# Seven block products in place of eight for the projection of v, z, q and k in a two-layer trunk

## The chip, the cores and the metric

One Trainium2 chip, one core of it, one launch. The metric is the device time of one execution in microseconds (us); the median of several runs is given, and one further execution was recorded by the hardware profiler.

## What is computed

Two layers, 512 tokens, width 1024. Per layer (cut from the reference):

```python
h = rms_norm(x, pre_norm[layer])
proj = h @ w_in[layer]                      # 1024 -> 8192 columns
c_b, c_c, c_x, c_z, r_q, r_k, r_v, r_z = split(proj)          # 1024 columns each
y_conv = c_b * causal_depthwise_conv(c_c * c_x, conv_w[layer]) * silu(c_z)
q, k = apply_rotary(r_q), apply_rotary(r_k)                   # 8 heads of 128
ret = retention_chunkwise(q, k, r_v, log_gamma)               # chunks of 128 tokens
ret = ret * rsqrt(mean(ret * ret) + eps)                      # per head
mix = concat(y_conv, ret * silu(r_z))                         # 2048
x = x + rms_norm(mix @ w_out[layer], post_norm[layer])
```

## The kernel before

Every operand of a product with a weight is split exactly into a high and a low part (`split`, L97: ScalarE writes the high part, VectorE subtracts it and writes the low part), and every product runs as three passes, high x high, high x low and low x high (`mm3`, L251 to L254). A weight unit is 256 rows by 512 columns (512 KB); one DMA brings it (`raw`), the split makes `wh` and `wl`, in three rotating buffers each. `prepare` (L129) splits units two ahead of the one that TensorE is at, and `fetch` (L116) asks for the load three ahead.

A layer goes through four pairs of heads, then the output projection. A pair has four runs of 96 matmuls, each of 128 x 128 by 512 columns:

- [v z], with the tokens as the stationary operand (4 token tiles, 8 slices of 128 rows, 3 passes). `take_vz` (L295) scales v on VectorE and takes SiLU of z on ScalarE.
- [q k], with the weight as the stationary operand, so that q and k come out with the head dimension on partitions. `rope` (L312) turns them by the rotary tables on VectorE.
- Two runs for two tiles of 128 channels of the convolution (`conv`, L421). Beside them TensorE does the retention's small products: `scores` (L334), `state` (L358), `attend` (L371). `state` wants k with tokens on partitions; `k_natural` (L348) makes that by 32 x 32 transposes on VectorE.

`finish` (L408) transposes the pair's result y in 16 pieces on VectorE and splits it into `mTh`, `mTl`; it is traced in the hooks of the next pair's [v z] run. The output projection (L551 on) takes `mTh`, `mTl` as the stationary operand. Between the layers, `transposed` (L476) turns the new x by TensorE and splits it.

Engines work in order, each on its own queue. The program is traced in the order of the text; the framework then places each engine's instructions in a queue, by the order of tracing among those that its plan finds ready. A hook is work traced behind a step of a run.

## Time and profile before

| | us |
|---|---|
| median of 3 runs | 943.01 (942.83 to 943.49) |
| span of the profiled execution | 941.0 |
| TensorE, VectorE, ScalarE, GpSimd busy | 933.1, 596.7, 278.4, 24.6 |
| one pair (from the first `pss` of pair 0 to that of pair 1, 62.54 to 156.04) | 93.5 |

Engines are named PE (TensorE matmul), PEld (its weight load), DVE (VectorE), ACT (ScalarE), POOL (GpSimd) and SP (the queue that issues most loads). A row of a group gives line, engine, operation, output and inputs, shapes and count, then busy time, the mean in ns of one, and the idle time ahead of it with what ended it. A row of a timeline gives start, duration, engine and line. Matmuls overlap in the records (one is about 390 ns long and a new one starts every 0.23 us), so the pace of TensorE is read from starts, not from durations. Times within a run are from the start of the span.

### The profile page before, as it was taken

Reading aid. Unit: us, or ns where it says so; the run is one execution under the profiler, and the core shown is the slowest. Engines: PE = TensorE matmul, PEld = TensorE weight load, DVE = VectorE, ACT = ScalarE, POOL = GpSimd, SP = SyncE. Lnnn points to the kernel's source line nnn. Section 1 sums busy time; section 2 is a strip of 40 time slices with the busy share of each in tenths; the row PEclk is TensorE's granted clock in tenths of the full one; section 3 lists DMA queues with packets and bytes.
Section 4 is the critical chain, followed back from the end, with each engine's and each line's share of the span. In section 5 each row is a group of like instructions: output and inputs, shape, how many; then the busy total and the mean of one; then the engine's idle time right before and its main releaser. Section 6 shows DMA issues by size and latency. Waiting matters only on the chain.

```text
span 941.0 us, 10986 instructions
## 1 busy us (share of the span) xinstructions
PE 933.1 (99%) x4338; PEld 776.0 (82%) x4338; DVE 596.7 (63%) x960; ACT 278.4 (30%) x450; POOL 24.6 (3%) x46
## 2 busy tenths in 40 slices
PE   9999999999999999999999999999999999999997
PEld 6788888888888888888888888888888888888886
DVE  5595839583958395825764948394849484947324
ACT  5522331222133213324542133213321332222311
POOL 0000000000000000000000000000000000000000
PEclk9999999999999999999999999999999999999999
DMA  8522132213222322235532222322222222222222
GB/s 309 178 92 90 53 127 90 90 63 116 90 90 68 112 90 90 71 108 179 178 122 103 91 90 79 100 90 90 88 92 90 90 90 90 90 91 90 89 68 90
DMA packets 27700, 96.60 MB, mean 103 GB/s; under 512 B 3328, under 2 KB 3456, under 8 KB 27648
## 3 DMA queue, kind: packets, MB, share of 16 engines
q1 hardware_dynamic: 27504, 95.88, 30.7%
q8 instruction: 34, 0.56, 0.2%
q14 instruction: 18, 0.15, 0.1%
q10 hardware_dynamic: 144, 0.01, 0.0%
HBM read 93.78 MB, written 2.10 MB: 102 GB/s over the span
## 4 chain that ended last, share of the span: by engine, by line
PE 94%; DMA 2%; DVE 1%; ACT 1%; issue 1%; POOL 0%; SPq 0%; DVEq 0%; POOLq 0%; ACTq 0%
PE mm L252 30%; PE mm L254 29%; PE mm L253 29%; PE pa L378 2%; PE pss L339 2%; PE pa L382 1%; PE pk L361 1%; DMA xT<-in_x_t 1%; DMA x<-in_x 1%; DVE wl L100 1%; DMA pre_c<-in_pre_norm 0%; DVE x L470 0%; PE psx L481 0%; ACT wh L99 0%; ACT jx L219 0%
## 5 line engine op out<-in xcount | busy, mean ns | idle before, releaser
L100 DVE TENSOR_TENSOR wl<-raw,wh 128x1024 fp32r<-128x1024 f32 (+1 forms) x169 | 205.4, 1217 | 226.5 <-ACT wh L99 222.8
L99 ACT ACTIVATE wh<-raw 128x1024 fp32r<-128x1024 f32 (+1 forms) x169 | 178.1, 1054 | 470.6 <-PE mm L253 303.1
L252 PE MATMUL mm<-hTh,wh 128*128 128x512 f32 x768 | 302.5, 394 | 0.1
L254 PE MATMUL mm<-hTh,wl 128*128 128x512 f32 x768 | 299.8, 390 | 0.3 <-DVE wl L100 0.3
L253 PE MATMUL mm<-hTl,wh 128*128 128x512 f32 x768 | 298.7, 389 | 0.0
L254 PEld LDWEIGHTS mm<-hTh,wl 128*128 128x128 f32 x768 | 144.1, 188 | 31.4 <-DVE wl L100 0.7
L252 PEld LDWEIGHTS mm<-hTh,wh 128*128 128x128 f32 x768 | 144.3, 188 | 29.3 <-ACT z L304 0.6
L253 PEld LDWEIGHTS mm<-hTl,wh 128*128 128x128 f32 x768 | 144.3, 188 | 29.1
L252 PE MATMUL mm<-wh,hTh 128*128 128x512 f32 x256 | 99.6, 392 | 0.3 <-ACT hTh L99 0.3
L253 PE MATMUL mm<-wl,hTh 128*128 128x512 f32 x256 | 99.8, 390 | 0.0
L254 PE MATMUL mm<-wh,hTl 128*128 128x512 f32 x256 | 99.8, 390 | 0.0
L252 PE MATMUL mm<-wh,mTh 128*128 128x512 f32 x256 | 99.8, 390 | 0.0
L254 PE MATMUL mm<-wh,mTl 128*128 128x512 f32 x256 | 99.6, 389 | 0.0
L253 PE MATMUL mm<-wl,mTh 128*128 128x512 f32 x256 | 99.6, 389 | 0.0
L252 PEld LDWEIGHTS mm<-wh,hTh 128*128 128x128 f32 x256 | 48.1, 189 | 11.5 <-ACT wh L99 1.2
L415 DVE STREAM_TRANSPOSE yT<-y 32x256 f32<-32x256 f32 x128 | 55.8, 436 | 2.1
L253 PEld LDWEIGHTS mm<-wl,hTh 128*128 128x128 f32 x256 | 48.1, 188 | 10.5 <-DVE wl L100 0.6
L254 PEld LDWEIGHTS mm<-wh,mTl 128*128 128x128 f32 x256 | 48.0, 188 | 10.1
L254 PEld LDWEIGHTS mm<-wh,hTl 128*128 128x128 f32 x256 | 48.1, 188 | 9.9
L252 PEld LDWEIGHTS mm<-wh,mTh 128*128 128x128 f32 x256 | 48.1, 188 | 9.9
L253 PEld LDWEIGHTS mm<-wl,mTh 128*128 128x128 f32 x256 | 48.1, 188 | 9.9
L356 DVE STREAM_TRANSPOSE kn<-qk 32x192 f32<-32x192 f32 x128 | 47.3, 370 | 2.0
(85 smaller groups left out, 596.3 us busy)
## 6 DMA issues: line engine op xcount, KB each, us to landing
raw<-in_w_in SPq DMA_DIRECT2D x127, 512.0 KB, 3.3
raw<-in_w_out SPq DMA_DIRECT2D x40, 512.0 KB, 3.3
x<-in_x SPq DMA_DIRECT2D x4, 512.0 KB, 7.2
out<-x SPq DMA_DIRECT2D x8, 256.0 KB, 2.1
xT<-in_x_t SPq DMA_DIRECT2D x3, 512.0 KB, 7.7
post<-in_post_norm SPq DMA_DIRECT2D x2, 512.0 KB, 5.5
xT<-in_x_t SPq DMA_DIRECT2D x2, 256.0 KB, 3.9
raw<-in_w_in SPq DMA_DIRECT2D x2, 256.0 KB, 4.2
```

The lines of the kernel that those rows point to most:

```text
L99: nc.scalar.activation(out=dst_h, in_=src, func=AF.Copy)
L100: nc.vector.tensor_tensor(out=dst_l, in0=src, in1=dst_h.bitcast(F32), op=ALU.subtract)
L252: nc.tensor.matmul(out=ps, lhsT=ah, rhs=bh, start=first, stop=False)
L253: nc.tensor.matmul(out=ps, lhsT=ah, rhs=bl, start=False, stop=False)
L254: nc.tensor.matmul(out=ps, lhsT=al, rhs=bh, start=False, stop=last)
L339: nc.tensor.matmul(out=pss[:, j, :], lhsT=self.kT[:, h, s], rhs=self.qT[:, h, s], start=True, stop=True)
L356: nc.vector.transpose(out=self.kn[cols, :, :, rows], in_=src[rows, :, : NT - 1, cols])
L361: nc.tensor.matmul(out=pk[:, h, :], lhsT=self.kn[:, h, t, :], rhs=self.vs[t][:, h, :], start=True, stop=True)
L378: nc.tensor.matmul(out=pa[:, j, :], lhsT=self.sT[b][:, j, :], rhs=self.vs[t][:, h, :], start=True, stop=(t == 0))
L382: nc.tensor.matmul(out=pa[:, j, :], lhsT=self.qT[:, h, t * P : (t + 1) * P], rhs=self.S[t][:, h, :], start=False, stop=True,)
L415: nc.vector.transpose(out=self.yT[rows, :, :, cols], in_=self.y[cols, :, :, rows])
```

## The change

[v z] and [q k] of a pair become one product of a 2 x 2 block matrix (tokens in halves of 256, input rows in halves of 512) by another (input rows in halves, [v z] and [q k] as column halves), done by seven block products (Strassen's scheme) instead of eight. A block product is 24 matmuls (2 token tiles, 4 slices, 3 passes) and takes two weight entries of 12 matmuls each; a pair has 14 such entries in place of 8 of 24.

- Four of the seven take a sum of weight blocks; VectorE builds it in place in the loaded buffer (`sums` in `prepare`), ahead of the split. Fourteen entries per pair are split instead of eight. There are ten loads instead of eight, in nine rotating load buffers.
- Four take a sum of blocks of the normalised tokens; `block_sums` builds and splits these once per layer.
- Results are combined out of PSUM: three copies by ScalarE (`R[1]`, `R[7]`, `R[2]`), three additions by VectorE.
- q and k now come out with tokens on partitions. `rope` works per token tile on strided views, `k_natural` goes, and `turn` makes the transposed q and k: per token tile four transposes on TensorE into a bank of PSUM and one copy by ScalarE.
- `take_vz` is on ScalarE alone. The splits of the mixer's result move from `finish` and `conv` into `parts`, between the units of the output projection.
- In the first pair of layer 0 the first two block products need half of the tokens; `second_tokens` scales and splits the rest behind them.
- The residual x leaves its buffers: it is written out (`keep_x`) in layer 1's first pair and read again (`load_x`) ahead of the output projection; `post` is loaded there too.
- PSUM: three double banks for products and two single ones for the rest, in place of five and three.

The diff, cut:

```diff
+    mm = ctx.enter_context(tc.tile_pool(name="mm", bufs=1, space=PSUM))
+    aux = ctx.enter_context(tc.tile_pool(name="aux", bufs=2, space=PSUM))
...
+    FIRST = ("p2", "p1", "p7", "p6", "p5", "p4", "p3")
+    OTHER = ("p1", "p7", "p6", "p2", "p5", "p4", "p3")
...
+                    if prod == "p1":
+                        blk[11, u] = load(w_in[l, g, u])
+                        entry(prod, [blk[11, u]], [], blk[11, u])
+                    elif prod == "p2":
+                        blk[21, u] = load(w_in[l, g, 2 + u])
+                        entry(prod, [blk[21, u]], [], blk[21, u])
+                    elif prod == "p7":
+                        blk[12, u], blk[22, u] = load(w_in[l, g + 1, u]), load(w_in[l, g + 1, 2 + u])
+                        entry(prod, [blk[12, u], blk[22, u]], [(blk[22, u], blk[12, u], "add", blk[22, u])], blk[22, u])
+                    elif prod == "p6":
+                        entry(prod, [], [(blk[22, u], blk[11, u], "subtract", blk[22, u])], blk[22, u])
+                    elif prod == "p5":
+                        entry(prod, [], [(blk[11, u], blk[11, u], "subtract", blk[12, u])], blk[11, u])
+                    elif prod == "p4":
+                        entry(prod, [], [(blk[22, u], blk[22, u], "add", blk[21, u])], blk[22, u])
+                    else:
+                        j = load(w_in[l, g + 1, 2 + u])
+                        entry(prod, [j], [], j)
...
+            ls, sums, src = entries[i]
+            for dst, a, op, b in sums:
+                nc.vector.tensor_tensor(out=raws[dst], in0=raws[a], in1=raws[b], op=getattr(ALU, op))
             wh = wpool.tile([P, 2, 512], F32R, name=f"wh{i}", tag="wh")
             wl = wpool.tile([P, 2, 512], F32R, name=f"wl{i}", tag="wl")
...
+                split(wh, wl, raws[src])
             ws[i] = (wh, wl)
...
+    def block_sums(l, raw, Sh, Sl):
+        def blk(i, j):
+            return raw[:, 4 * (j - 1) : 4 * j, 256 * (i - 1) : 256 * i]
+        def parts(f, src):
+            split(Sh[:, f], Sl[:, f], src)
+        nc.vector.tensor_tensor(out=blk(2, 2), in0=blk(2, 2), in1=blk(2, 1), op=ALU.subtract)
+        nc.vector.tensor_tensor(out=blk(2, 1), in0=blk(2, 1), in1=blk(1, 1), op=ALU.subtract)
+        parts(1, blk(2, 1))
+        nc.vector.scalar_tensor_tensor(
+            out=blk(1, 1), in0=blk(2, 2), scalar=-1.0, in1=blk(1, 1), op0=ALU.mult, op1=ALU.subtract
+        )
+        parts(2, blk(1, 1))
+        parts(0, blk(2, 2))
+        nc.vector.tensor_tensor(out=blk(1, 2), in0=blk(1, 1), in1=blk(1, 2), op=ALU.add)
+        parts(3, blk(1, 2))
...
+        where = dict(p1=W, p6=W, p5=W, p3=W, p2=X, p7=Y, p4=Y)
...
+        def behind(prod):
+            if prod == "p1":
+                R[1] = copy("r1", W, "qk", padded_shape=[P, 4, 512])
+            elif prod == "p7":
+                R[7] = copy("r7", Y, "R", bufs=2)
+            elif prod == "p6":
+                R[2] = copy("r2", W, "R", bufs=2)
+            if prod in ("p1", "p2") and prod != order[0]:
+                nc.vector.tensor_tensor(out=R[1], in0=X, in1=R[1], op=ALU.add)
+            if prod == ("p2" if order[0] == "p1" else "p7"):
+                first_vz()
+            if prod == "p5":
+                nc.vector.tensor_tensor(out=R[7], in0=W, in1=R[7], op=ALU.add)
+                O[1] = rope(l, p, 1, R[7])
+            elif prod == "p4":
+                nc.vector.tensor_tensor(out=R[2], in0=Y, in1=R[2], op=ALU.add)
+                take_vz(l, p, 1, R[2], *VZ, *factors())
+            elif prod == "p3":
+                O[0] = rope(l, p, 0, W)
...
+        for prod in order:
+            base = at[l, p, prod]
+            for u in range(2):
+                wh, wl = ws[base + u]
+                for t in range(2):
+                    for kk in range(2):
+                        k = 2 * u + kk
+                        ah, al = operand(prod, k, t)
+                        first = prod in ("p1", "p2", "p7") and k == 0
+                        mm3(where[prod][:, t, :], ah, al, wh[:, kk, :], wl[:, kk, :], first, k == 3,
+                            prod in ("p6", "p5", "p3", "p4"))
+                step_done(base + u + 1)
+                for fn in hooks.get((prod, u), ()):
+                    fn()
+            behind(prod)
+        banks.extend((tags[1], tags[2], tags[0]))
+        return *VZ, O
...
+        def turn(self, t):
+            ps = aux.tile([P, 4, P], F32, name=f"pt_{self.tag}_{t}", tag="aux")
+            for j in range(4):
+                nc.tensor.transpose(
+                    out=ps[:, j, :], in_=self.O[t // 2][:, t % 2, j * P : (j + 1) * P], identity=ident
+                )
+            nc.scalar.activation(out=self.qkT[:, :, t * P : (t + 1) * P], in_=ps, func=AF.Copy)
...
+    def second_tokens():
+        for k in range(NK):
+            for half in (1, 0):
+                s = slice(256 * half, 256 * half + 256)
+                nc.scalar.activation(
+                    out=xT[:, k, s], in_=xT[:, k, s], func=AF.Copy, scale=pre_c[:, 0, k : k + 1]
+                )
+        for half in range(2):
+            ks = slice(4 * half, 4 * half + 4)
+            split(hTh0[:, ks, 256:], hTl0[:, ks, 256:], xT[:, ks, 256:])
...
+                    hooks["p2", 0] = [load_rest]
+                    hooks["p2", 1] = [second_tokens]
+                    hooks["p1", 0] = [lambda: block_sums(0, raw, Sh, Sl)]
+                    hooks["p7", 0] = [lambda t=t: square_sum(0, t) for t in range(NT)] + [lambda: set_factors(0)]
+                    hooks["p6", 0] = [rotary_tables]
+                else:
+                    hooks["p2", 0] = [lambda: emit(2, 0), lambda: emit(3, 0)]
+                    hooks["p2", 1] = [lambda: emit(2, 1), lambda: emit(3, 1), lambda: block_sums(1, raw, Sh, Sl)]
+                    hooks["p7", 0] = [lambda t=t: square_sum(1, t) for t in (2, 3)] + [lambda: set_factors(1)]
+                    hooks["p7", 1] = [lambda t=t: keep_x(t) for t in range(NT)]
+                hooks["p5", 0] = [lambda l=l: set_rows(l)]
+            else:
+                prods = order_of(l, p)
+                for i in range(4):
+                    hooks[prods[i // 2], i % 2] = [lambda r=done, a=i: r.finish(a)]
+            V, Z, O = seven(l, p, hTh, hTl, Sh, Sl, hooks, lambda: (fac["rx"], fac["vt"]))
+            if m is None:
+                m = [area(t, f"m{l}_{t}", [P, 8, SEQ], F32) for t in tags["m"]]
+            ret = Retention(l, p, V, Z, O, fac["et"], m)
...
+                0: [lambda t=t: ret.turn(t) for t in (2, 3, 0, 1)],
+                1: [lambda: ret.scores(0)],
+                2: [lambda: ret.scores(1)],
```

## Rows read from the trace of the kernel before

**Rows 1.** The page: busy time per engine, and the chain that ended last by engine.
```profile
PE 933.1 (99%) x4338; PEld 776.0 (82%) x4338; DVE 596.7 (63%) x960; ACT 278.4 (30%) x450; POOL 24.6 (3%) x46
...
PE 94%; DMA 2%; DVE 1%; ACT 1%; issue 1%; POOL 0%; SPq 0%; DVEq 0%; POOLq 0%; ACTq 0%
```

**Rows 2.** Waits: who waited for whom, us in total, times, longest.
```profile
PE mm L254 <- DVE wl L100: 0.3, 1, 0.3
```

**Rows 3.** Timeline of PE, 159.7 to 163.6: start, us, engine, line, operation.
```profile
159.77 0.39 PE L253 MATMUL mm<-hTl,wh 128*128 128x512 f32 x1
...
162.03 0.40 PE L254 MATMUL mm<-hTh,wl 128*128 128x512 f32 x1
...
163.08 0.48 PE L252 MATMUL mm<-hTh,wh 128*128 128x512 f32 x1
163.39 0.39 PE L253 MATMUL mm<-hTl,wh 128*128 128x512 f32 x1
```

**Rows 4.** The chain of waits, whole run: start, us, what.
```profile
62.54 0.89 PE pss L339 x8
...
156.04 0.89 PE pss L339 x8
...
455.60 0.88 PE psx L481 x8
```

**Rows 5.** Groups of instructions by shape: count, busy us, mean ns, idle before.
```profile
L100 DVE TENSOR_TENSOR wl<-raw,wh 128x1024 fp32r<-128x1024 f32 x167 | 204.1, 1223 | 226.5 <-ACT wh L99 222.8
L99 ACT ACTIVATE wh<-raw 128x1024 fp32r<-128x1024 f32 x167 | 176.8, 1059 | 470.6 <-PE mm L253 303.1 <-PE mm L254 99.4 <-issue 66.0
L323 DVE TENSOR_TENSOR qk<-t,t 128x512 f32<-128x512 f32 x32 | 22.1, 692 | 0.8
L304 ACT ACTIVATE z<-mm,rx 128x256 f32<-128x256 f32 x32 | 14.4, 472 | 20.8 <-DVE v L299 20.8
L299 DVE TENSOR_TENSOR v<-mm,vt 128x256 f32<-128x256 f32 x32 | 13.0, 421 | 11.4 <-PE mm L254 11.2
```

**Rows 6.** Stretches: busy (count) per engine, granted clock, DMA share, GB/s.
```profile
5.50:51.60 46.10, 45.62 (x198) 36.46 (x198) 27.89 (x44) 23.90 (x35) 1.29 (x2) 1.00 0.66 239
16.00:30.00 14.00, 14.00 (x63) 11.61 (x62) 4.90 (x7) 7.93 (x12) 1.16 (x1) 1.00 0.96 351
101.60:123.40 21.80, 21.80 (x98) 18.06 (x97) 18.47 (x32) 7.74 (x10) 0.10 (x1) 1.00 0.29 97
123.40:145.10 21.70, 21.70 (x97) 17.96 (x97) 8.41 (x10) 4.74 (x6) 0.00 (x0) 1.00 0.30 98
450.00:472.00 22.00, 22.00 (x107) 18.37 (x106) 17.19 (x23) 13.46 (x18) 1.10 (x2) 1.00 0.53 168
472.00:517.50 45.50, 45.22 (x209) 37.28 (x208) 24.23 (x37) 15.36 (x25) 1.67 (x3) 1.00 0.34 116
932.00:941.00 9.00, 3.03 (x14) 2.18 (x12) 5.17 (x10) 1.38 (x4) 1.09 (x2) 0.83 0.47 175
```

**Rows 7.** Timeline of DVE about the end of a pair (195.1).
```profile
141.76 0.68 DVE L320 TENSOR_TENSOR t<-mm,cos_t 128x512 f32<-128x512 f32 x1
...
192.96 1.12 DVE L403 SCALAR_TENSOR_TENSOR y<-pa,ra,z 128x128 f32<-128x128 f32 x4 [1.12 <-POOL ra L396]
...
195.60 0.42 DVE L415 STREAM_TRANSPOSE yT<-y 32x256 f32<-32x256 f32 x1
195.96 0.64 DVE L433 TENSOR_TENSOR pb<-mm,row 128x512 f32<-128x512 f32 x1
...
203.51 4.50 DVE L415 STREAM_TRANSPOSE yT<-y 32x256 f32<-32x256 f32 x10
208.04 1.23 DVE L100 TENSOR_TENSOR wl<-raw,wh 128x1024 fp32r<-128x1024 f32 x1
```

**Rows 8.** Timeline of the start: first product, last part of the transposed x.
```profile
5.50 0.98 PE L252 MATMUL mm<-wh,hTh 128*128 128x512 f32 x2
...
13.85 1.34 ACT L103 ACTIVATE hTh<-xT,pre_c 128x512 fp32r<-128x512 f32 x2 [0.21 <-DMA xT<-in_x_t]
```

More of the change, by code (lines that the diff above doesn't have):

```diff
@@ L52 @@
 C_INVF = 0
-C_MASK = C_INVF + 1
+C_MASK = C_INVF + HD // 2
 C_ID = C_MASK + P
@@ new lines, in area, with load, entry @@
+    def area(tag, name, shape, dtype):
+        return hpool.tile(shape, dtype, name=name, tag=tag)
+    loads, entries, last_use = [], [], {}
+    def load(src):
+        loads.append(src)
+        return len(loads) - 1
+    def entry(name, ls, sums, src):
+        i = len(entries)
+        entries.append((ls, sums, src))
+        for j in list(ls) + [a for t in sums for a in t if isinstance(a, int)] + [src]:
+            last_use[j] = i
+        return i
+    FIRST = ("p2", "p1", "p7", "p6", "p5", "p4", "p3")
@@ new lines, in hybrid_trunk, with fetch @@
+    NRAW = 9
+    raws, ws = {}, {}
+    with_load = {0: [(2, 0)], 1: [(3, 0)], 2: [(0, 0)], 3: [(1, 0)], 4: [(0, 1), (1, 1), (2, 1), (3, 1)]}
+    def fetch(limit):
+        done = len(ws) - 1
+        while len(raws) < len(loads):
+            j = len(raws)
+            if first_use[j] > limit or (j >= NRAW and last_use[j - NRAW] > done):
+                return
+            raws[j] = wpool.tile([P, 2, 512], F32, name=f"raw{j}", tag="raw", bufs=NRAW)
+            parts = range(2) if j == 0 else (slice(0, 2),)
+            for kk in parts:
+                for kp, half in with_load.get(j, ()):
+                    if j == 0:
+                        nc.sync.dma_start(out=xT[:, 2 * kp + kk, :256], in_=x_t[kp, half, :, kk, :])
+                    else:
+                        nc.sync.dma_start(
+                            out=xT[:, 2 * kp : 2 * kp + 2, 256 * half : 256 * half + 256], in_=x_t[kp, half]
+                        )
+                nc.sync.dma_start(out=raws[j][:, kk, :], in_=loads[j][:, kk, :])
@@ L248, in factor_rows, with mm3, bank, step_done @@
         return row, row2
-    def mm3(ps, ah, al, bh, bl, first, last):
-        nc.tensor.matmul(out=ps, lhsT=ah, rhs=bh, start=first, stop=False)
-        nc.tensor.matmul(out=ps, lhsT=ah, rhs=bl, start=False, stop=False)
-        nc.tensor.matmul(out=ps, lhsT=al, rhs=bh, start=False, stop=last)
+    def mm3(ps, ah, al, bh, bl, first, last, more=False):
+        nc.tensor.matmul(out=ps, lhsT=ah, rhs=bh, start=first, stop=False, skip_group_check=more)
+        nc.tensor.matmul(out=ps, lhsT=ah, rhs=bl, start=False, stop=False, skip_group_check=more)
+        nc.tensor.matmul(out=ps, lhsT=al, rhs=bh, start=False, stop=last, skip_group_check=more)
     cursor = [0]
+    banks = ["mm0", "mm1", "mm2"]
+    def bank(name):
+        tag = banks.pop(0)
+        return tag, mm.tile([P, 2, 512], F32, name=name, tag=tag)
+    def step_done(i):
+        cursor[0] = i
+        prepare(i + 2)
     def run_units(steps, targets, operands, hooks=None):
@@ L270, in run_units @@
                             u == 0 and kk == 0, u == n - 1 and kk == 1)
-            cursor[0] = base + min([u for later, _ in steps[i + 1 :] for u in later], default=n)
-            prepare(cursor[0] + 2)
+            step_done(base + min([u for later, _ in steps[i + 1 :] for u in later], default=n))
             for fn in (hooks or {}).get(i, ()):
                 fn()
+        banks.extend(tag for tag, _ in pairs)
         return [ps[t] for t in targets]
@@ new lines, in take_vz @@
+    def take_vz(l, p, half, src, V, Z, rx, vt):
+        for i in range(2):
+            t = 2 * half + i
+            for h in range(2):
+                s = slice(h * HD, (h + 1) * HD)
+                nc.scalar.activation(
+                    out=V[:, t, s], in_=src[:, i, s], func=AF.Copy, scale=vt[:, t, 2 * p + h : 2 * p + h + 1]
+                )
+            nc.scalar.activation(
+                out=Z[:, t, :], in_=src[:, i, 256:512], func=AF.Silu, scale=rx[:, t : t + 1]
+            )
@@ L299, in take_vz, with rope @@
+    def rope(l, p, half, src):
+        o = xpool.tile([P, 2, 512], F32, name=f"o_{l}_{p}_{half}", tag=f"x{2 + half}")
+        H = HD // 2
+        for i in range(2):
+            t = 2 * half + i
+            t1 = tpool.tile([P, 4, 2, H], F32, name=f"t1_{l}_{p}_{t}", tag="cc")
+            t2 = tpool.tile([P, 4, 2, H], F32, name=f"t2_{l}_{p}_{t}", tag="sz")
+            s4 = src[:, i, :].rearrange("p (g a d) -> p g a d", g=4, a=2)
             nc.vector.tensor_tensor(
-                out=v, in0=ps[t][:, 0:256].rearrange("p (h d) -> p h d", d=HD),
```

321 lines of the change are left out of this document (165 added, 156 removed).

## The prediction

> **What bounds the kernel now.** I read the page first. TensorE is busy 99% of the span and the chain is TensorE's to 94% [rows 1]; the waits hold nothing of weight on its side (0.3 us for a low part of a weight, once) [rows 2]. So the time is TensorE's queue, and its pace is read from starts: 10 matmuls from 159.77 to 162.03, 0.227 us each [rows 3]. The kernel has 3840 of them, 872 of 941 us. The span is 941.0, the median 943.0; 2.0 us lie around the span, and I add them at the end.
>
> VectorE has 597 busy us, 63% [rows 1], but in waves. Where a pair begins (101.6) it is busy 18.5 of 21.8 us, with the convolution's rest and `finish` of the pair ahead; then 8.4 of 21.7 [rows 6]. TensorE doesn't notice, since a unit is 24 matmuls, 5.4 us, and a split asks 1.22 us of VectorE. The change works in just these stretches.
>
> **TensorE's own sum.** Removed: 24 matmuls per pair, 192 in all, x 0.227 = 43.6 us. Added: 128 transposes in 32 calls of `turn`. The nearest row is the same operation between the layers: 8 of them 0.88 us, 0.11 each [rows 4], so 14.1 us; behind such a group the first matmul takes 0.31 instead of 0.227 [rows 3], up to 2.6 us more for 32 groups. I take 16 us, 2.0 a pair. ScalarE's copies of 512 columns out of two banks may hold up the third and fourth `turn`, a few tenths; the matmuls of the convolution stand behind. Net -27.6 us: a span of 913.4 if TensorE never waits.
>
> The page "TensorE: Matmul & The Clock Gate" of the Trainium skill, Part 4, gives about 275 ns for a transpose in a kernel's context. By it 128 would be 35 us as an estimate, and the total 19 us above mine; the row's 0.11 us is a pace, and I keep it.
>
> **VectorE in an ordinary pair (six of eight).** The 14 entries of the block product take TensorE 168 x 0.227 = 38.1 us. What must VectorE do until the last is split? From 101.6 to 145.1 it was busy 26.9 us [rows 6]. Away go: v's scaling, 4 x 0.42 = 1.7 [rows 5]; the splits of the mixer's result, 0.69 + 1.22 = 1.9 (they move to the output projection, below); rope's start from 141.76 on, 3.2 [rows 7]. Come in:
> - six more splits, 6 x 1.22 = 7.3 [rows 5];
> - eight sums of weights. No row has this very operation; `wl` has its shape, its two inputs and its engine, 1.22 [rows 5], so 9.8;
> - two of the three additions that combine (128 x 1024), 2.4;
> - rope of tokens 256 on, which is traced ahead of the last entry's split: two tiles x (0.69 + 2 x 0.42 + 0.69) = 4.4 [rows 5].
>
> Sum 26.9 - 6.8 + 23.9 = 44.0 us against 38.1. That is 5.9 too many. The two sums of p7 depend on loads alone and may run in the stretch before, where VectorE is idle half the time: 3.5 left. Neighbours that don't depend on each other overlap by some 0.09 us, which takes 1.4 off 16 of them; waits like the 1.12 us for GpSimd [rows 7] put as much back. Can it slip? A split waits for one of three buffers, so it can't run more than two entries (5.4 us) ahead; what can be put off is `finish`, 16 x 0.45 = 7.2 [rows 7], but the rows show the queue put it early: a transpose stands ahead of the convolution's product at 195.60, and ten in a row ahead of a `wl` that was ready long since (208.04) [rows 7]. That cost nothing with 5.4 us per unit; with 2.7 per entry, of which sum and split take 2.4, it does. I take 4.2 us of waiting (bounds 0 and 8: all fits, or neither p7's sums nor the overlap help). A pair: -5.4 + 2.0 + 4.2 = +0.8; six, +4.8 (-20 to +27).
>
> ScalarE, 14 splits x 1.06, three copies and v, z, comes to some 23 of 38 us [rows 5]: no bound, but it stands between a sum and its low part.
>
> **Layer 1's first pair.** From 472.0 to 517.5 VectorE had 24.2 busy us [rows 6]. To that come 7.3 + 9.8 + 2.4 + 4.4 as above, and `block_sums`, four sums and four splits of 1024 columns, 8 x 1.22 = 9.8; away go v, 1.7, and rope's start, 3.2. 53.0 us, where TensorE has 38.1 + 1.8 for the old transposes. With 1.5 us of waits in the chain of transposes, sums and splits the stage takes 54.5 instead of 45.5: +9.0, and 2.0 for `turn`: +11 (+4 to +16). `keep_x` puts four writes on SP's queue behind loads asked for four entries ahead; v of this pair waits for them on ScalarE, with splits behind it. Price 0 to 3 us, in the bounds.
>
> **Layer 0's first pair.** The first two products need tokens 0 to 255 and start as before at 5.5 [rows 8] and lose as much at the start (2.6 us: 240 matmuls, 54.4 us, lie before the first `pss` at 62.54 [rows 4]), so they end at 19. p7 needs a sum over all tokens. The last of x came at 13.9 [rows 8], with 3.5 MB asked for; in the new order some 4 MB, at about 15. Then ScalarE scales 16 pieces of 256 columns, 16 x 0.47 = 7.5 (z's row has this size and a scale by partition) [rows 5], between splits, to 22; two splits, high 1.06 and low 1.22, to 24.5; two sums to 27; the high part to 28. TensorE stands still from 19 to 28. From 27 VectorE still has 6 of the 8 block operations, six sums and eight splits (7.3 + 7.3 + 9.8), one addition, rope 4.4, and rotary tables and factors of some 5: 35 us, so the last split comes at 62 and the stage ends at 65, where [q k] ended at 51.6 (48 matmuls before that `pss`). By the same account as above: 27.9 busy [rows 6] + 33.7 - 7.7 = 54 from 5.5 with 4 to 5 idle, the same. +14, with `turn` +16 (+8 to +25).
>
> **The rest.** `parts` in the output projection: eight splits per layer where a unit of 24 matmuls leaves VectorE 4 us; nothing, with `finish` there as before. Its cover would be gone only with units of 12. Layer 1's new x is turned two steps later, four groups in 8.2 us with three splits, 5.5 + 3.7 of work: +1 (0 to 3). Loads: 16 more of 512 KB, x twice more and written once, 15 MB on 97. The start moved 351 GB/s, the pair stages under 100 [rows 6]; the densest new place is the output projection's second half with x's reload. It had 168 GB/s [rows 6]; 2.6 MB over 22 us make 290. Hidden, and `post`, now behind `finish` on SP's queue, is wanted 10 us later.
>
> **Sum.** 4.8 + 11 + 16 + 1 = +32.8 on 941.0: a span of 973.8, and 975.8 with what lies around it. 976.
>
> **Rivals.**
> 1. Hidden after all: VectorE's 44 us come down to 38, which needs 6 us per pair taken out of the stretch (finish and p7's sums done before it, rope behind the last split). For it: the stretch to 145.1 has 13 idle us in 21.7. Against it: three buffers, and a queue that puts such work first. Then only the layers' first pairs wait, about half as long: 915.4 + 1 + 5 to 15 = 921 to 931, faster. It decides where all waiting together is under 27 us; the two first pairs as I count them make 34 by themselves (14 + 5.4 and 9 + 5.4), so they would have to shrink as well.
> 2. The chain, not the work: sum (VectorE), high part (ScalarE), low part (VectorE), with VectorE idle in the 1.06 us between. Eight per pair, 8.5 us, 68 in all. For it: VectorE waited 223 us for ScalarE's half before [rows 5]; against it: when it lags, there is a next sum to fill in. Half of it gives 1010, all 1044.
> 3. In between: ordinary pairs stall 2 us, the first ones as I say less a third: 976 - 13 - 9 = 954 and down to 940.
> 4. The clock. In the last 9 us, where TensorE has work in 3.0 only, the granted clock is 0.83 [rows 6]. If it fell to the half in layer 0's standstill, each matmul behind it would cost 0.23 more: 24 of them 5.4 us, 981. It is inside the forecast's range. The same page of the Trainium skill, Part 1, has the gate throttle an idle engine; whether 9 us here do it no row shows.
>
> That the change doesn't do what it says is no case of its own: the diff fixes the count of matmuls.
>
> **Chances.** Forecast 0.65 (own range 955 to 1000; the clock lies in it), hidden 0.14, in between 0.1, the chain 0.11. The range 935 to 1008 leaves out the hidden case and, of the chain, what is above half of it. Less than 0.2% (1.9 us) the measurement can't tell from no change. Faster: 0.14 and half of the case in between, 0.19; same 0.03; slower 0.78.
>
> **What would show it.** Pair to pair (first `pss` to first `pss`) 94.3 instead of 93.5 [rows 4]; TensorE idle some 4 us in the block product of ordinary pairs, ended by `wl`, and VectorE near 9 tenths through it; TensorE idle about 9 us before p7 in layer 0. Matmul starts 0.227 apart outside the waits, 8 transposes about 0.9 us. It is wrong if the pair period is near 90 with VectorE idle there, or if VectorE waits long for ScalarE's half while TensorE waits too.

## The result and the profile after

| | before | after |
|---|---|---|
| median, us | 942.9 (942.6 to 943.5) | 988.5 (986.5 to 988.9) |
| span of the profiled execution, us | 941.0 | 986.8 |
| ordinary pair, first `pss` to first `pss`, us | 93.5 | 95.4 |

The ratio of the times is 1.048, with an interval of 1.0464 to 1.0495. The change makes the kernel 4.8% slower. 976 was forecast, in a range of 935 to 1008.

The page of the changed kernel: busy time per engine, the granted clock in 40 slices of the span, the chain that ended last.

```profile
PE 932.5 (94%) x4274; PEld 761.8 (77%) x4274; DVE 683.1 (69%) x949; ACT 398.9 (40%) x637; POOL 26.2 (3%) x46
...
PEclk9799999999999999999988999999999999999998
...
PE 75%; DVE 16%; ACT 4%; issue 3%; POOL 1%; DMA 1%; SPq 0%; DVEq 0%; POOLq 0%; ACTq 0%
```

TensorE had 94% of the chain [rows 1]; it has 75% now, and VectorE 16%. TensorE lost 192 matmuls, got 128 transposes and is as long busy as before: a busy figure doesn't tell the pace, and part of its work ran at half clock (below). To see where the 45.8 us of span lie, one looks for the same mark in both kernels. Timeline of PE, the first `pss` of pair 3 in layer 0 and of pair 0 in layer 1, before:

```profile
342.89 0.38 PE L339 MATMUL pss<-qk,qk 128*128 128x128 f32 x2
...
528.22 0.61 PE L339 MATMUL pss<-qk,qk 128*128 128x128 f32 x4
```

and after, with those of pairs 0 and 1 of layer 0 ahead of them:

```profile
83.29 0.94 PE L550 MATMUL pss<-qkT 128*128 128x128 f32 x7
178.69 0.49 PE L550 MATMUL pss<-qkT 128*128 128x128 f32 x3
...
369.69 0.49 PE L550 MATMUL pss<-qkT 128*128 128x128 f32 x3
571.42 0.49 PE L550 MATMUL pss<-qkT 128*128 128x128 f32 x3
```

| term | forecast | measured | from |
|---|---|---|---|
| layer 0's first pair | +16 | +15.3 | block product ends at 64.9 instead of 51.6 [rows 6]; `turn` 2.0 |
| six ordinary pairs | +4.8 | +11.6 | 95.4 instead of 93.5 |
| layer 1's first pair, with the new x | +12 | +16.4 | 201.7 between the marks instead of 185.3 |
| behind the last matmul | 0 | +2.2 | 8.6 us instead of 6.35 |
| sum | 32.8 | 45.5 | of 45.8 |

**An ordinary pair.** Its block product starts at 117.08 and ends at 160.28: 43.2 us, for 168 matmuls worth 38.1. Timeline of PE in it, the four waits and what follows them:

```profile
128.82 0.50 PE L346 MATMUL ps<-wl,Sh 128*128 128x512 f32 x1 [0.46 <-DVE wl L105]
...
132.12 0.51 PE L345 MATMUL ps<-wh,Sh 128*128 128x512 f32 x1 [0.47 <-ACT wh L104]
...
133.07 0.49 PE L345 MATMUL ps<-wh,hTh 128*128 128x512 f32 x1 [0.44 <-ACT wh L104]
...
134.50 0.50 PE L346 MATMUL ps<-wl,Sh 128*128 128x512 f32 x1 [0.94 <-DVE wl L105]
...
135.49 0.63 PE L346 MATMUL ps<-wl,Sh 128*128 128x512 f32 x1
135.91 0.63 PE L347 MATMUL ps<-wh,Sl 128*128 128x512 f32 x1
...
138.47 0.40 PE L347 MATMUL ps<-wh,Sl 128*128 128x512 f32 x1
138.71 0.40 PE L346 MATMUL ps<-wl,hTh 128*128 128x512 f32 x1
```

With the restarts behind them the waits make 3.6 us, all at the fifth to seventh of the fourteen entries (the 50th and the 61st to 63rd of the 168 matmuls); no wait of weight follows in the stage. Behind them eight matmuls start 0.42 us apart instead of 0.23: TensorE at the lower of its two clock levels, 1.5 us more. Timeline of VectorE ahead of the same waits:

```profile
124.79 1.22 DVE L215 TENSOR_TENSOR raw<-raw,raw 128x1024 f32<-128x1024 f32 x1
125.92 0.69 DVE L645 TENSOR_TENSOR m_E<-acc,sz 128x512 f32<-128x512 f32 x1
126.62 0.88 DVE L619 STREAM_TRANSPOSE m_E<-y 32x256 f32<-32x256 f32 x2
127.54 1.23 DVE L105 TENSOR_TENSOR wl<-raw,wh 128x1024 fp32r<-128x1024 f32 x1
128.79 0.89 DVE L619 STREAM_TRANSPOSE m_E<-y 32x256 f32<-32x256 f32 x2
129.69 1.22 DVE L215 TENSOR_TENSOR raw<-raw,raw 128x1024 f32<-128x1024 f32 x1
130.95 2.24 DVE L619 STREAM_TRANSPOSE m_E<-y 32x256 f32<-32x256 f32 x5
133.22 2.36 DVE L105 TENSOR_TENSOR wl<-raw,wh 128x1024 fp32r<-128x1024 f32 x2
```

The convolution's last step (L645), `finish` (L619), weight sums (L215) and splits (L105) stand in one queue. At 130.95 five transposes, for which nobody waits yet, stand ahead of the low parts of the sixth and seventh entry; for the first of them TensorE waits until 134.50. Twelve of the 16 transposes come in the block product before these low parts.

**The first pair of a layer.** Timeline of PE, the standstills (the first four lines are layer 0, the others layer 1):

```profile
20.66 0.39 PE L347 MATMUL ps<-wh,hTl 128*128 128x512 f32 x1
31.37 0.80 PE L345 MATMUL ps<-wh,Sh 128*128 128x512 f32 x1 [10.32 <-ACT Sh L104]
...
45.48 0.39 PE L347 MATMUL ps<-wh,Sl 128*128 128x512 f32 x1
47.95 0.50 PE L345 MATMUL ps<-wh,Sh 128*128 128x512 f32 x1 [2.07 <-ACT r L445]
...
505.34 0.40 PE L347 MATMUL ps<-wh,hTl 128*128 128x512 f32 x1
515.23 0.79 PE L345 MATMUL ps<-wh,Sh 128*128 128x512 f32 x1 [9.49 <-ACT Sh L104]
...
530.26 0.39 PE L347 MATMUL ps<-wh,Sl 128*128 128x512 f32 x1
534.07 0.52 PE L345 MATMUL ps<-wh,hTh 128*128 128x512 f32 x1 [3.43 <-ACT wh L104]
```

In both layers p7 waits for `Sh`, the high part of its own block sum, which is the second that VectorE makes. In layer 1 VectorE makes that sum at 512.87 and is busy without a pause from 502.4 until then, with the new x, its low parts, a weight sum and an addition that combines. In layer 0, p5 follows p6 on the same bank of PSUM and waits for ScalarE's copy of it (2.07). In layer 1, a weight's high part waits on ScalarE (3.43); ScalarE's timeline shows behind what:

```profile
529.46 1.05 ACT L104 ACTIVATE wh<-raw 128x1024 fp32r<-128x1024 f32 x1
532.17 0.91 ACT L500 ACTIVATE z<-r,rx 128x256 f32<-128x256 f32 x2 [1.66 <-POOL rx L323]
532.98 1.04 ACT L104 ACTIVATE wh<-raw 128x1024 fp32r<-128x1024 f32 x1
```

z stands ahead of the split and waits for `rx`, which GpSimd makes from the square sums that ScalarE itself wrote until 529.5.

### The profile page after: what moved, and what is told of

Its sections match the earlier page's. It is cut to its first block, busy times and chain, and to the rows that moved or that the text cites. A ratio compares the mean times of both kernels' runs of the same rounds, so it can differ in the third digit from the quotient of the medians.

```text
span 986.8 us, 11141 instructions
## 1 busy us (share of the span) xinstructions
PE 932.5 (94%) x4274; PEld 761.8 (77%) x4274; DVE 683.1 (69%) x949; ACT 398.9 (40%) x637; POOL 26.2 (3%) x46
## 4 chain that ended last, share of the span: by engine, by line
PE 75%; DVE 16%; ACT 4%; issue 3%; POOL 1%; DMA 1%; SPq 0%; DVEq 0%; POOLq 0%; ACTq 0%
PE mm L347 16%; PE mm L346 16%; PE mm L345 16%; PE ps L346 7%; PE ps L347 6%; PE ps L345 6%; DVE wl L105 4%; ACT wh L104 2%; PE pa L581 2%; DVE raw L215 1%; PE pss L550 1%; PE pa L586 1%; DVE m_C L619 1%; DVE m_E L619 1%; PE pk L563 1%
## 5 line engine op out<-in xcount | busy, mean ns | idle before, releaser
L105 DVE TENSOR_TENSOR wl<-raw,wh 128x1024 fp32r<-128x1024 f32 (+1 forms) x217 | 262.6, 1217 | 154.1 <-ACT wh L104 135.1
L345 PE MATMUL mm<-hTh,wh 128*128 128x512 f32 x512 | 203.8, 398 | 0.0
L347 PE MATMUL mm<-hTh,wl 128*128 128x512 f32 x512 | 201.2, 393 | 0.0
L346 PE MATMUL mm<-hTl,wh 128*128 128x512 f32 x512 | 199.5, 390 | 0.0
L345 PE MATMUL ps<-wh,Sh 128*128 128x512 f32 x256 | 107.5, 420 | 26.3 <-ACT Sh L104 20.9
L346 PE MATMUL ps<-wl,Sh 128*128 128x512 f32 x256 | 107.2, 419 | 9.5 <-DVE wl L105 9.5
L347 PE MATMUL ps<-wh,Sl 128*128 128x512 f32 x256 | 105.3, 411 | 0.2 <-DVE Sl L105 0.2
L215 DVE TENSOR_TENSOR raw<-raw,raw 128x1024 f32<-128x1024 f32 x64 | 76.9, 1221 | 33.8 <-DMA raw<-in_w_in 33.8
L345 PE MATMUL mm<-wh,mh 128*128 128x512 f32 x256 | 99.8, 390 | 0.0
L347 PE MATMUL mm<-wh,ml 128*128 128x512 f32 x256 | 99.6, 389 | 0.0
L346 PE MATMUL mm<-wl,mh 128*128 128x512 f32 x256 | 99.6, 389 | 0.0
```

The costliest lines, as they stand in the source:

```text
L105: nc.vector.tensor_tensor(out=dst_l, in0=src, in1=dst_h.bitcast(F32), op=ALU.subtract)
L215: nc.vector.tensor_tensor(out=raws[dst], in0=raws[a], in1=raws[b], op=getattr(ALU, op))
L345: nc.tensor.matmul(out=ps, lhsT=ah, rhs=bh, start=first, stop=False, skip_group_check=more)
L346: nc.tensor.matmul(out=ps, lhsT=ah, rhs=bl, start=False, stop=False, skip_group_check=more)
L347: nc.tensor.matmul(out=ps, lhsT=al, rhs=bh, start=False, stop=last, skip_group_check=more)
```

## The experiments

Two theories of the ordinary pair were on record for the first runs, "work" (VectorE has too much to do until the last split) and "chain" (sum, high part, low part, one after the other on two engines). A third, "early peak" (what VectorE has to do ahead of the first consumers sets the wait, not its total), was formed after the first four runs. The diffs are cut; their lines are those of the changed kernel. Work that is traced later is not bound to run later: the framework's plan may put it ahead of other work as soon as its operands are ready, so where an instruction stands is read from the trace of each run.

**1. `finish` traced in the convolution run.** It goes behind steps 1 and 2 of the first convolution run.

```diff
-                    hooks[prods[i // 2], i % 2] = [lambda r=done, a=i: r.finish(a)]
+            late = [lambda r=done, a=a: r.finish(a) for a in range(4)] if done else []
...
+                1: [lambda: ret.scores(0)] + late[:2],
+                2: [lambda: ret.scores(1)] + late[2:],
```

> The 16 transposes of `finish` move from the block product of the next pair into its first convolution run; nothing else changes. Theory 'work': VectorE has 44 us to do in the 38.1 us of an ordinary pair's block product, and TensorE waits for the excess. Without the 7.2 us of `finish` it has 37, so the 3.6 us of waits in an ordinary pair go, and with them the 1.5 us at half clock: pair period 90.3 to 91.5 instead of 95.4, total 958 to 965. Rival 'chain': TensorE waits for the passage sum (VectorE), high part (ScalarE), low part (VectorE), which this leaves as it is: period 94 or more, total 980 or more. The first pairs of the layers keep their time under both.

972.97 us (ratio 1.0324, 1.0294 to 1.0354), above the 958 to 965 that "work" asked for. The block product takes 39.25 us: of the 5.1 lost, 1.2 is left, and no matmul in it runs at half clock. But the rest of the pair takes 53.2 instead of 52.2, and the period is 92.4. Timeline of VectorE in the block product of this run, from 118.04 to 157.30:

```profile
131.44 2.35 DVE L105 TENSOR_TENSOR wl<-raw,wh 128x1024 fp32r<-128x1024 f32 x2
...
138.36 1.78 DVE L619 STREAM_TRANSPOSE m_E<-y 32x256 f32<-32x256 f32 x4
...
144.74 3.15 DVE L619 STREAM_TRANSPOSE m_E<-y 32x256 f32<-32x256 f32 x7
```

The transposes did not leave the block product. 15 of the 16 are in it, as in the changed kernel, but only two ahead of the low parts of the sixth and seventh entry, where the changed kernel has twelve. Of the 52 instructions that VectorE starts in the changed kernel's block product, 51 are there too (the last one of `rope` moved behind it). So the run took no work away, as its expectation took for granted; it changed the order, and the order is worth 3.9 us of the stage. That falsifies "chain", whose sums and splits are all still there, and it speaks against "work" as well. What the total does is seen behind the stage: VectorE is busy 38.8 of its 39.3 us, and 0.9 of the microsecond that the rest of the pair loses are two waits for low parts, with their restarts, where the convolution's run begins. The first pairs of the layers, expected to keep their time, are longer by 1.0 and 2.2 us.

**2. More work for VectorE.** One more addition of 128 x 512, traced ahead of each weight sum, 0.685 us by its row, 5.5 us a pair.

```diff
             for dst, a, op, b in sums:
+                scr = tpool.tile([P, 512], F32, name=f"scr{i}", tag="scr")
+                nc.vector.tensor_tensor(out=scr, in0=raws[a][:, 0, :], in1=raws[b][:, 0, :], op=getattr(ALU, op))
```

> Ahead of each of the eight sums of weights of a pair VectorE does one more addition of 128 x 512 into a scratch tile (0.60 us each where it follows an independent one), 4.8 us a pair. Theory 'work': VectorE is full in these stretches, so nearly all of it shows: period 99.5 to 100.5, total 1020 to 1030. Rival 'chain': VectorE idles while ScalarE makes the high part, and the added work fits in there at least by half: period under 98, total under 1010.

990.45 us in one run. The ordinary periods are 94.4 to 95.6 and TensorE's idle time in the stage is 3.5 to 4.4 us, so the 99.5 us that "work" forecast didn't come. But the run doesn't test what it was made for. Timeline of VectorE, an addition in an ordinary block product (217.16 to 260.35) and one in the convolution's runs behind it:

```profile
240.47 0.69 DVE L216 TENSOR_TENSOR scr<-raw,raw 128x512 f32<-128x512 f32 x1
...
278.43 0.69 DVE L216 TENSOR_TENSOR scr<-raw,raw 128x512 f32<-128x512 f32 x1 [4.90 <-DMA raw<-in_w_in]
```

Six of a pair's eight additions run in the convolution's runs, where VectorE has room, and the other two at 23 and 30 us into the block product, behind the last early wait. Not one stands ahead of the waits, and the waits are the same (0.46, 0.47, 0.45, 0.93). So the run says nothing of the total or the peak in an ordinary pair. Two things it does show. In the three ordinary pairs where the clock stayed up the block product is 42.3 to 42.5 us, where run 3 has 42.0: of the 1.4 us of the two late additions 0.3 to 0.5 show. And in layer 0's first pair all eight additions are in the block product, which takes 65.2 us, against 59.8 in the changed kernel and 60.1 to 61.0 in runs 1, 3, 5 and 11: there most of the added 5.5 us shows.

**3. Keeping TensorE busy in the standstill.** 40 matmuls of zeros ahead of p7 in each layer's first pair.

```diff
+            if p == 0 and prod == "p7":
...
+                for _ in range(40):
+                    nc.tensor.matmul(out=pz, lhsT=zz[:, :P], rhs=zz[:, :512], start=True, stop=True)
```

> In the first pair of each layer 40 products of zeros (128 x 512, 8.7 us) stand on TensorE's queue ahead of p7, where it waited 10.3 and 9.5 us. Theory: the granted clock falls to the half because TensorE stood still; with the dummies p7 starts as late as before, but at the full clock, and the 8 to 10 matmuls at 0.425 us behind each standstill take 0.227: 1.5 to 2 us less in layer 0, 1 to 2 in layer 1, total 984 to 987 by the same measure as the 988.5 of the changed kernel. Rival: what comes next is late anyway (VectorE's work sets the time), and the clock costs nothing: total within 1 us. Rival: the dummies themselves delay p7: total up by some us.

986.19 us (1.0465, 1.0415 to 1.0515), not told apart from the changed kernel. In layer 0 the matmuls are back at 0.23 us apart at 34.2 instead of 36, but the block product ends at 65.7, no earlier than 64.9: the later waits for ScalarE's copy and for weights take the gain. So the half clock behind layer 0's standstill is not on the path. The profiled span is 4.5 us shorter mostly for another reason: in three of the six ordinary pairs the half clock hardly appears, and their block product takes 42.0 instead of 43.2. In layer 1 the block product takes 58.8 instead of 60.6, but without the zeros it is anywhere from 59.1 to 62.2 in runs 1, 2, 5 and 11, so a gain there is not shown.

**4. First pairs by eight plain products.** The first pair of each layer multiplies [v z] and [q k] as before; `block_sums` moves into its [q k] run, with the second pair the first to need it. The loads of layer 0's x go back to their old order. Of the diff only the call is shown.

```diff
-            V, Z, O = seven(l, p, hTh, hTl, Sh, Sl, hooks, lambda: (fac["rx"], fac["vt"]))
+            if p == 0:
+                V, Z, O = eight(l, p, hTh, hTl, raw, Sh, Sl)
+            else:
+                V, Z, O = seven(l, p, hTh, hTl, Sh, Sl, hooks, lambda: (fac["rx"], fac["vt"]))
```

> The first pair of each layer does its eight products plainly (tokens stationary, 192 matmuls, no sums); the sums of tokens for the later pairs are made during its [q k] run. Theory: the first pairs lose 21.3 and 20.7 us to waits and half clock because the sums of tokens and weights stand between their operands and TensorE; plainly they take 43.5 us plus 2.6 at the start of layer 0 and plus 2 of transposes in layer 1, so 13 to 14 us less in layer 0 and 13 to 15 less in layer 1: total 959 to 963. Rival: the sums only move and hold up the rest of the pair: a gain under 15 us, total over 973.

962.57 us (1.0214, 1.0184 to 1.0244). The first `pss` comes at 72.3 instead of 83.3 and the distance across the layers is 187.6 instead of 201.7; the other periods are 95.2 to 95.4 as before. 25 of the 45.8 us are gone with the scheme in the two first pairs alone.

**5. The same work, later.** `finish` is issued behind p2 and p5, the fourth and fifth product; VectorE's work in the stage is the same.

```diff
-                    hooks[prods[i // 2], i % 2] = [lambda r=done, a=i: r.finish(a)]
+                    hooks[prods[3 + i // 2], i % 2] = [lambda r=done, a=i: r.finish(a)]
```

> The four finish steps of the previous pair are issued behind the steps of p2 and p5 (the fourth and fifth product) in place of those of p1 and p7 (the first two). VectorE has exactly the same work in the block product, only later. Theory 'early peak' (TensorE waits at the third to sixth entry because the conv's rest, the finish and the first sums come at once, and VectorE has room behind them): the stage falls from 43.2 to 39-40 us and the pair period from 95.5 to 91-92.5, without the microsecond that the move into the conv's run cost there; time 960-970. Rival 'total of the stage' (VectorE's sum of work up to the last split sets the stage, as the prediction counted it): nothing is gained, period 95-96, time 984-990.

973.74 us (1.0324, 1.0308 to 1.0339). The block product takes 39.46, the pair 92.7, so the rest of it takes 53.2 as in the first run: that microsecond is no price of a place in the convolution's run, against what was expected; in neither run did `finish` stand there. It shows as short waits where that run begins (0.3 us for a low part, once in each ordinary pair, and a shorter one ahead of it). Layer 1's first pair is a little longer (203.2 instead of 201.7). The stage in four stretches: busy time and count of PE, PEld, DVE, ACT, POOL, granted clock, DMA share, GB/s; the changed kernel first, then this one.

```profile
117.08:127.00 9.92, 9.92 (x45) 8.24 (x44) 9.72 (x15) 4.61 (x5) 0.10 (x1) 1.00 0.01 2
127.00:135.00 8.00, 5.69 (x21) 3.59 (x21) 7.78 (x13) 4.08 (x5) 0.00 (x0) 1.00 0.00 1
135.00:139.00 4.00, 4.00 (x13) 3.09 (x12) 3.91 (x6) 0.09 (x1) 0.00 (x0) 0.57 0.00 0
139.00:160.28 21.28, 21.28 (x95) 17.59 (x94) 19.04 (x22) 13.35 (x21) 0.00 (x0) 1.00 0.72 248
```

```profile
117.54:127.50 9.96, 9.96 (x45) 8.26 (x44) 9.83 (x14) 4.59 (x5) 0.10 (x1) 1.00 0.01 2
127.50:135.50 8.00, 7.33 (x32) 5.74 (x31) 7.96 (x9) 4.35 (x5) 0.00 (x0) 1.00 0.42 132
135.50:139.50 4.00, 4.00 (x19) 3.33 (x18) 3.87 (x7) 2.56 (x3) 0.00 (x0) 1.00 0.42 145
139.50:157.00 17.50, 17.38 (x77) 14.05 (x76) 17.29 (x25) 8.84 (x17) 0.00 (x0) 1.00 0.60 208
```

VectorE is full in the second stretch of both (7.78 and 7.96 of 8). Over the whole stage it has the same instructions but for one, and is busy 40.45 of 43.20 and 38.95 of 39.46 us. What differs is what it does in the second stretch: 21 matmuls run beside transposes, 32 beside sums and splits. That is "early peak", and it was on record before the run, while "total of the stage" asked for a period of 95 to 96. The total is not far behind, though: with the peak gone VectorE is busy for 99% of the stage. With the waits the half clock goes too (0.57 to 1.00).

**6 and 7. Both cures together**, first with `finish` behind p2 and p5, then traced behind the last step of the first and the first step of the second convolution run. The second, against the fourth run (`late` as in run 1):

```diff
-                2: [lambda: ret.scores(1)],
+                2: [lambda: ret.scores(1)] + late[:2],
...
-                0: [lambda: ret.state(0), lambda: ret.state(1), lambda: ret.attend(0)],
+                0: [lambda: ret.state(0), lambda: ret.state(1)] + late[2:] + [lambda: ret.attend(0)],
```

> Both cures together: the first pair of each layer by eight plain products, and the finish steps of the others behind p2 and p5. If the two losses are independent, their gains add: 988.5 less the 26 of the plain first pairs less six times 3 to 4 = 938-945, so about level with the kernel before (942.9). If the one only moves the other's wait, 955-963.

> As the one before, but the finish steps go behind the last step of the first conv tile (two) and the first step of the second (two), where VectorE is busy for 1.7 of 4 us at a time. Theory 'early peak': stage 39, period 90.5-92, time 935-943. Rival: the conv's own work on VectorE, which frees the accumulator, is pushed back by the finish, so that TensorE waits at the next run's start: period 93-95, time 948-958.

947.5 (1.0044, 1.003 to 1.0058) and 945.9 (1.0029, 1.0017 to 1.0041). The gains add: 988.5 less 25.9 less 6 x 2.7 is 946.4. Both lie a little above what was expected, since the period came to 92.7 and 92.45, not to 91 or 92. The rest of the pair is 53.2 in both. Run 7 is no trial of a place in the convolution's runs: as in run 1, 15 of the 16 transposes are in the block product, 13 of them from 20.3 us on, so the two runs differ little in VectorE's order.

**8. Weight sums on GpSimd.**

```diff
-                nc.vector.tensor_tensor(out=raws[dst], in0=raws[a], in1=raws[b], op=getattr(ALU, op))
+                nc.gpsimd.tensor_tensor(out=raws[dst], in0=raws[a], in1=raws[b], op=getattr(ALU, op))
```

> The eight weight sums of a pair are done by GpSimd in place of VectorE; the rest as in the changed kernel. If only VectorE's early work sets the wait, the stage falls towards 39-40 us and the time to 965-975, provided that GpSimd adds 128x1024 in less than about 5 us. If GpSimd's own duration is longer than the lead of two entries (about 9.5 us), or the two engines slow each other down, it rises to 1000 and over.

1033.8 us in one run, period 98.3 to 99.4. GpSimd's sum takes 2.60 us, well under 5, and yet it is slower by far: beside GpSimd's sums VectorE's own instructions get longer. Timeline of VectorE beside GpSimd's sums (137.3 to 142.5 and 144.3 to 149.8):

```profile
137.75 2.50 DVE L639 SCALAR_TENSOR_TENSOR acc<-u,cw,acc 128x512 f32<-128x512 f32 x1
140.28 0.44 DVE L619 STREAM_TRANSPOSE m_E<-y 32x256 f32<-32x256 f32 x1
140.75 2.31 DVE L639 SCALAR_TENSOR_TENSOR acc<-u,cw,acc 128x512 f32<-128x512 f32 x1
142.98 1.21 DVE L105 TENSOR_TENSOR wl<-raw,wh 128x1024 fp32r<-128x1024 f32 x1
...
147.53 3.37 DVE L105 TENSOR_TENSOR wl<-raw,wh 128x1024 fp32r<-128x1024 f32 x1
```

A convolution step of 0.74 us takes 2.50 and 2.31 and a low part of 1.22 takes 3.37, while a transpose of one tensor keeps its 0.44. The page "SBUF — State Buffer" of the Trainium skill, "SBUF: two separate sides", says that VectorE and GpSimd hold one pair of ports in turn, for a whole instruction, when VectorE has two inputs in SBUF; these rows agree. How much of the 45 us this makes was not taken apart: 16.6 of them are layer 0's block product (76.4 instead of 59.8), and in five of the six ordinary ones TensorE stays at half clock twice as long.

**9. The start of layer 0.** In the seventh run ScalarE scaled xT for the block sums ahead of the second to fourth weight; here these scalings keep their place behind.

```diff
-            nc.scalar.activation(out=xT[:, k, :], in_=xT[:, k, :], func=AF.Copy, scale=pre_c[:, 0, k : k + 1])
+            xs = nc.scalar.activation(out=xT[:, k, :], in_=xT[:, k, :], func=AF.Copy, scale=pre_c[:, 0, k : k + 1])
+            tc.keep_in_program_order(xs)
```

> The version with plain first pairs and the finish steps in the conv runs, with one thing more: ScalarE's eight scalings of xT in layer 0 (needed for the block sums alone, some 50 us later) are kept behind the weights' splits, where the planner had put them ahead of the second to fourth entry. TensorE's waits of 1.62 and 0.53 us at 11.5 to 14.8 us and of 0.60 at 36 us should go: 945.9 less 2.5 = 943.4, level with the kernel before. If the block sums now come late for the second pair's p7, a new wait appears there and it stays at 945-947.

944.75 us (1.0018, 1.001 to 1.0027), an interval that overlaps the seventh run's. The wait of 1.62 fell to 0.48, the one of 0.53 stayed, the one of 0.60 went: half of what was hoped. In the traces the first `pss` comes at 71.5 instead of 72.4.

**10. Half a microsecond off the peak.** The convolution's first tap goes to ScalarE.

```diff
-        nc.vector.tensor_scalar(
-            out=acc, in0=u[:, 0:SEQ], scalar1=cw[:, l, 0, ct : ct + 1], scalar2=None, op0=ALU.mult
-        )
+        nc.scalar.activation(out=acc, in_=u[:, 0:SEQ], func=AF.Copy, scale=cw[:, l, 0, ct : ct + 1])
```

> As the one before, and the conv's first tap (a multiplication by one factor per channel, 0.49 us on VectorE) is done by ScalarE. It takes 0.5 us of VectorE's work out of the stretch ahead of the fifth entry, where TensorE still waits 0.7 us in each ordinary block product. Theory 'early peak': the wait falls to 0.2-0.4 us, the period from 92.45 to 91.8-92.1, time 939-942, under the kernel before. Rival: ScalarE is busy with a split when the tap comes, the conv's chain gets longer, and the accumulator is freed later: period 92.5-93.5, time 943-950.

941.73 us (0.9988, 0.9978 to 0.9997). The period falls from 92.45 to 91.95, half a microsecond for half a microsecond, one half of it in the block product (39.27 to 39.0), the other where the convolution's run begins. The number came as expected, the step did not: the wait at the sixth entry fell from 0.71 to 0.62, not to 0.2 to 0.4, since VectorE's queue put one more transpose of `finish` where the tap had been. VectorE is busy 38.6 of the 39.0 us. So the gain fits VectorE's total, now that the peak is spread out, better than the early wait that was named.

**11. The end.** Timelines of TensorE and ScalarE behind the last matmuls of the changed kernel:

```profile
978.22 0.39 PE L347 MATMUL mm<-wh,ml 128*128 128x512 f32 x1
```

```profile
978.71 0.60 ACT L664 ACTIVATE j<-mm 128x512 bf16<-128x512 f32 x1 [3.19 <-PE mm L347]
...
980.34 0.60 ACT L664 ACTIVATE j<-mm 128x512 bf16<-128x512 f32 x1 [0.94 <-DVE og L667]
```

The square sum of token tile 2, whose last matmul started at 975.5, waits until tile 3 is finished, and tile 3's waits in turn for VectorE's reading of tile 2: two tiles in one double bank. Here the last two get single banks.

```diff
...
+        for t in targets[len(targets) - single :]:
+            ps[t] = aux.tile([P, 512], F32, name=f"mm{base}_s{t}", tag="aux")
...
```

> The changed kernel, with the last run of the second layer's output projection writing its last two token tiles into single banks of PSUM instead of one double bank; nothing else. In the changed kernel ScalarE's square sum of tile 2 waits until tile 3 is finished too, and the tail behind TensorE's last matmul is 8.6 us instead of 6.35. Theory 'shared bank': the tail falls back to about 6.4 us, the span by 2.2, the time from 988.5 to 986.3. Rival (the tail is longer for another reason, the post-norm's operands): nothing moves, 988.5.

986.41 us (1.0466, 1.0451 to 1.048). The median is the expected one, but that is luck: the interval overlaps the changed kernel's, and the trace agrees only by half, with a tail of 7.5 us instead of 8.6. Tiles 0 and 1 still share a double bank, so VectorE gets to the last two late (the square sum of tile 2 is done at 974.2, VectorE goes on with it at 975.9). The profiled span is 3.5 us shorter, the rest of it mostly because the half clock hardly appears in four of the ordinary pairs. The shared bank is shown for 1.1 of the 2.2 us; for the other half it is the likely cause, not a tried one.

**12. All cures together.**

> The version with the plain first pairs, the finish steps in the conv runs, the conv's first tap on ScalarE, and the last two tiles in single banks. 941.7 less 2.2 = 939.5, that is 0.36% under the kernel before (938.5 to 940.5). If the tail does not shrink here, 941.7.

939.87 us (0.9971, 0.996 to 0.9983): 0.29% faster than the kernel before, and 4.9% faster than the changed one. Its page and two marks of PE's timeline:

```profile
PE 921.9 (98%) x4322; PEld 758.8 (81%) x4322; DVE 635.7 (68%) x897; ACT 386.3 (41%) x625; POOL 25.2 (3%) x46
```

```profile
70.41 0.49 PE L557 MATMUL pss<-qkT 128*128 128x128 f32 x3
...
162.35 0.49 PE L557 MATMUL pss<-qkT 128*128 128x128 f32 x3
```

The pair is down to 91.9, 1.6 under the kernel before, six times. Of these 9.7 us the layers' boundary takes back 2.3 (`turn` among them), the tail 1.3, the rest is layer 0's first pair. VectorE's share, 68%, hardly differs from the changed kernel's 69%, with 47 us less work in a shorter span.

## Why the forecast held, and where its steps failed

The side was right, and so was the ground named for it: TensorE ends up waiting for VectorE's sums and splits, and the first pair of a layer, where the block sums are made, costs more than it saves. 12.5 us were missing: 6.8 in the ordinary pairs, 4.4 in layer 1's first pair and 2.2 behind the last matmul, less 0.7 in layer 0's.

**TensorE's own sum** was right. The matmuls are 0.227 us apart outside the waits. The eight transposes from 171.17 to 171.93 start 0.11 us apart, as in the sum. The 275 ns of the Trainium skill ("TensorE: Matmul & The Clock Gate", Part 4) agree with the length of one of them in the trace, 0.27 us; as a pace the measurement decides against them. The pair outside the block product grew by 2.2 (52.2 against 50.0) where 2.0 was forecast.

**The ordinary pair**: +1.9 instead of +0.8. The price of a weight sum was right (1.221 by its row, 1.22 taken). Of the 4.2 us of waiting, 3.6 came, but not by the step that gave them, so that the size came right is partly luck. "What must VectorE do until the last is split" made 44.0 against 38.1 us, as if the stage filled up evenly. The count itself was good: without p7's two sums, which did run earlier, it leaves 41.6, and VectorE was busy 40.4. But it was busy for that in 43.2 us, with nearly 3 to spare, while TensorE waited. All waits lie at the fifth to seventh entry of fourteen; runs 1 and 5 leave VectorE's work where it is, change its order and take most of the waits away. What decides is VectorE's queue from the convolution's end to the seventh entry, `finish` in it. The prediction had that in hand ("the rows show the queue put it early") and said that it would cost; it priced it by the whole stage all the same. The total comes second: with the order mended, some 2 us a pair are still lost, VectorE is full, and half a microsecond less work gains half a microsecond (run 10). The term that was missing is the clock: 1.5 us a pair at half clock behind the waits, or 1.2 against the pairs of run 3 where the clock stayed up, seven to nine in all. It was weighed for layer 0's long standstill alone.

**Layer 0's first pair**: +15.3 instead of +16, a stage end at 64.9 where 65 was said, p7 at 31.4 where 28 was said. The 3.4 us later start was made up behind it, as VectorE had less to do than the account had it: 50.9 busy us where it counted 54. So two errors cancelled in the end of the stage. Run 3, where the matmuls behind p7's start are nearly 2 us earlier and the end is not, and run 2, where 5.5 us more work in this block product made it some 5 us longer, agree with the sum in that VectorE's work sets the end. p5's wait for the copy of p6 was not foreseen; what it costs by itself was not tried.

**Layer 1's first pair**: +16.4 instead of +12. The step was "1.5 us of waits in the chain of transposes, sums and splits". The trace has 9.5 before p7, and later 3.4 for a split behind z on ScalarE's queue. It was priced by VectorE's total of 53.0 once more, while p7 needs only what stands in VectorE's queue from the new x to its block sum, and that queue is full from 502.4 to 514.1. A split queued behind a waiting v was in the bounds, for another cause (`keep_x`).

**The rest**: the out-projection at nothing was right for the splits, but the double banks at its end were not looked at: +2.2, of which run 11 shows 1.1.

**The rivals.** "Hidden" fell. It asked for work out of the stretch; the later runs only put `finish` behind the stretch's first consumers and took the scheme out of the first pairs, and that is worth most of the 49 us between the changed kernel and run 12. "The chain" fell with run 1. "The clock" in layer 0 came as described, half speed after the standstill (25.8 to 36.0), and run 3 shows no cost of it in the end of the stage.

## What to carry to other kernels

When an operand gets ready in half the time, look for the peak of the engine that prepares it, not for its total: list its queue from the stage's start to the first consumers, and move what nobody waits for behind them. Then look in the trace whether it moved, since a plan may put it back or put it elsewhere; here the queue undid the move in runs 1 and 7 and put most of run 2's work elsewhere. When the peak is spread out, the total is the next bound. A scheme that saves multiplications needs its sums early; where a stage begins with fresh data (the first pair of each layer here) the plain product may be faster, and the scheme can start one stage later. And look at the end of the program whenever tiles are put together in one buffer.

## What the runs showed of the hardware

- The granted clock fell although TensorE had been at work for most of the time: after four waits of 0.44 to 0.94 us between 128.4 and 134.5, eight matmuls ran 0.42 us apart, at the lower of its two levels (mean granted clock 0.57 from 135 to 139). In three ordinary pairs of the third run and four of the eleventh the waits were much the same (3.6 to 3.9 us) and the clock stayed up; their block product is 1.2 us shorter. When it falls was not settled.
- A sum of two tensors on GpSimd stretches VectorE's instructions with two SBUF inputs to as much as three times their length (0.74 to 2.50, 1.22 to 3.37 us), and leaves transposes of one input alone.
